# Four-tile pairs in another order of work, and an earlier table read on the DMA-issuing engine, in a ragged self-attention kernel

## The chip, the cores and the metric

The kernel runs on one core of one Trainium2 chip. The metric is device time in microseconds (us) for one execution. A core has a matrix engine (TensorE, PE), a vector engine (VectorE, DVE), a scalar engine (ScalarE, ACT), a general engine (GpSimd, POOL) and an engine that here only issues transfers (SyncE, SP). Each runs its own instruction stream; they meet through semaphores. PE writes only to PSUM, which this kernel divides into eight banks.

## The reference

32 sequences of 512 rows by 512 columns, each with a length between 64 and 511; 8 heads of 64 columns. Rows beyond a sequence's length are zero in the output.

```python
for b in range(batch):
    x_b = x[b, :lengths[b]]
    q, k, v = np.split(x_b @ w_qkv, 3, axis=-1)        # per head: (rows, 64)
    scores = scale * q @ k.T
    attn = softmax(scores)
    output[b, :lengths[b]] = (attn @ v)
```

The lengths are drawn once. Sorted and put in pairs, the longer length of each of the 16 pairs, rounded up to the next class (multiples of 32, and 340), is: 512, 448, 384, 352, 352, 340, 320, 288, 256, 224, 224, 192, 160, 160, 128, 96. In tiles of 128 rows that is four tiles for pairs 0 and 1, three for pairs 2 to 7, two for pairs 8 to 13 and one for pairs 14 and 15. No pair has class 480 or 416.

## The kernel before, in words

The sequences are sorted by length on the chip, and worked off in pairs from the longest. There is one straight piece of code per class and engine; a pair runs the code of its class, and branches lead from one class to the next. A body has two halves, `h` = 0 and 1. Half `h` does the attention of sequence `h` and, between its steps, the projections of the other buffer's sequence, that is of the one that comes next. Everything is done with two buffers of `xT`, `qkT`, `v_aug` and `onat`.

`half` (from L682) writes the order of a half out by hand, as a line of tokens. What they do:

- `S`: the scores of one pair of heads (a unit `i`, 0 to 3) against one 128-row tile of keys: two matmuls over 64 rows of the array (the two heads lie in the upper and the lower 64 rows), into one of two PSUM slots `s0`, `s1` in turn. ACT then writes the exponential to `ep` (L346) and frees the slot. The units come in the order 1, 2, 3, and 0 of the next sequence; with four tiles that is 16 `S`.
- `Qi`, `Ki`: a projection of unit `i` for the next sequence, four matmuls over 128 rows into one bank; capital letters let DVE move it to `qkT` (L410), small ones ACT (L409).
- `Ei` and then `Fi`, `Gi`, `Hi` or `Ii`: the same two projections, Q and K of unit `i`, in two banks at once, with matmuls over 64 rows: `E` (`cross_begin`) adds the upper rows into one bank and the lower rows into the other, the later token (`cross_end`) the rest. With `G`, DVE moves Q and ACT moves K.
- `Vi`: the value projection of row tile `i`, four matmuls of 512 columns over 128 rows; DVE moves it (L433).
- `Ai` (`attnv`): attention times values of unit `i`. DVE then takes the reciprocal of the row sums (L610) and multiplies (L629, L631) into `onat`. A `+` mixes its matmuls evenly into those of the token before.
- `O`: ACT issues the store of the first half of the columns. SP issues that of the second half.

A bank is free for the next writer once the engine that empties it has signalled; `acquire` puts that wait into PE's stream. Bodies with three tiles take the four banks `a0`, `a1`, `v0`, `v1` in turn (`in_turns`, L842), for projections and `A` alike. Bodies with four tiles use `a0`, `a1` for projections, and `v0` with `v1` together for `A`, in this order (L672):

```python
4: "S S Q0 +A0 S S K0 V0 S S Q1 +A1 S S K1 V1 S S Q2 +A2 S S K2 V2 S S Q3 +A3 S S V3 K3 O",
```

PE's bodies begin at chosen places of its instruction blocks (`align`, with the slots `FIRST` and `SECOND`), and hints announce branches.

SP's body of a class waits in each half until PE has begun it (`s_xtf`), issues the transposes of the next `x` into `xT[h]`, the store of the half before, and the load of an `x` five sequences ahead. Which sequences these are it reads from a small table, four registers a row (`read_step`, L1460). A body of two tiles has a branchless form for all but the last such pair (`steady`, L1464; pairs 8 to 12): one read at the top of the body (in `body`), and one between the halves (L1472).

Of the kernel before, what the change touches and what calls it, by code (L numbers as in the profile page):

```python
# [13 lines left out]
P = 128  # L14
NH = 8
HD = 64
# [7 lines left out]
SECOND = {4: 20, 3: AGAIN, 2: 0, 1: None}  # L24
AT_DENSE = 20
FIRST_DENSE = 4
PIECE = 266
PIECE_DENSE = 274
DENSE_ROWS = 340
# [121 lines left out]
def kernel(  # L151
# [9 lines left out]
    B, MAXS, D = x.shape  # L161
# [32 lines left out]
    rank = sb("rank", [B, 1], FP32)  # L194
# [11 lines left out]
    steps = sb("steps", [1, B, 4], I32)  # L206
# [4 lines left out]
    rcp = sb("rcp", [P, NPAIR, 4 * NPAIR], FP32)  # L211
# [332 lines left out]
            return  # L544
        group(pr, b, "dve", v_mms(b, h, i, T, of), v_out(b, h, i, T, of))

    def attnv(pr, h, i, T, late=False, b=None):

        for s_ in ("s0", "s1"):
            if pr.pair[s_] == i or T == 1 and pr.pair[s_] is not None:  # L550
                acquire(pr, s_)
        for v in halves_av if b is None else (b,):
            acquire(pr, v)
        va = v_aug[h]
        if b is not None:
            jobs = [(2 * 74 * qt, i, qt) for qt in range(T)]
        elif T == 1:
            jobs = [(74 * 2 * j, j, 0) for j in range(NPAIR)]
        elif T == 4:
            jobs = [(256 * qt, i, qt) for qt in range(T)]  # L560
        else:
            jobs = [(74 * (4 * qt + 2 * (i % 2)), i, qt) for qt in range(T)]
        mms = []
        for o0, j, qt in jobs:
            for par in range(2):
                o = o0 + par * (HD + 1 if T == 4 else 74)
                into = pav if b is None else area[b]
                for kt in range(T):
                    mms.append(
                        mm(  # L570
                            into[:, o : o + HD + 1],
                            ep[:, j, par, kt, qt * P : (qt + 1) * P],
                            va[:, kt, 2 * j + par, :],
                            kt == 0,
                            kt == T - 1,
                        )
                    )
        if b is None and T in (2, 3) and i % 2 == 0:
            acquire_carry(pr, mms)
            return  # L580
        on = onat[h]
        if b is not None:
            res = into[:, 0 : 2 * 74 * T].rearrange("p (t a d) -> p t a d", a=2, d=74)
            dst = on[:, i // 2, 0:T, P * (i % 2) : P * (i % 2 + 1)]
            dst = dst.rearrange("p t (a d) -> p t a d", d=HD)
            sh, fin = [T, 2], i % 2 == 1
        elif T == 4:
            res = pav.rearrange("p (j n) -> p j n", n=256)[:, :, 0 : 2 * (HD + 1)]
            res = res.rearrange("p j (a d) -> p j a d", d=HD + 1)
            dst = on[:, i // 2, :, P * (i % 2) : P * (i % 2 + 1)]  # L590
            dst = dst.rearrange("p t (a d) -> p t a d", d=HD)
            sh, fin = [NT, 2], i % 2 == 1
        else:
            sh, fin = [2, 4] if T == 1 else [T, 4], True
            res = pav[:, 0 : 74 * sh[0] * 4].rearrange("p (b j d) -> p b j d", j=4, d=74)
            if T == 1:
                dst = on[:, :, 0, :].rearrange("p b (j d) -> p b j d", d=HD)
            else:
                dst = on[:, i // 2, 0:T, :].rearrange("p t (a d) -> p t a d", d=HD)
        rv = rcp[:, i, 0 : sh[0] * sh[1]].rearrange("p (j a) -> p j a", a=sh[1])  # L600
        num, den = res[..., 0:HD], res[..., HD]
        name = "av" if b is None else b
        close(pr, name, "dve", mms, False)
        each = T == 4 or b is not None

        def recip():
            for j in (0, 1) if T == 1 else (i // 2,) if not each or i % 2 == 0 else ():
                pr.take("dve", s_od[h][j], 16)
            pr.take("dve", full[(name, "dve")])
            pr.add("dve", lambda e: e.reciprocal(out=rv, in_=den).then_inc(s_r, 1))  # L610

        def mult():
            pr.take("dve", s_r)

            if T == 1:
                cuts = [(slice(0, 2), 0)]
            elif h == 0:
                cuts = [(slice(0, T - 1), None), (slice(T - 1, T), T - 1)]
            else:
                cuts = [(slice(t, t + 1), t) for t in range(T)]  # L620

            def fn(e):
                for w, t in cuts:
                    ops = dict(
                        out=dst[:, w], in0=num[:, w],
                        in1=rv[:, w].unsqueeze(3).broadcast_to(list(num[:, w].shape)),
                    )
                    if t is None:
                        ins = e.tensor_tensor(op=ALU.mult, **ops)  # L629
                    else:  # L630
                        ins = e.scalar_tensor_tensor(  # L631
                            scalar=now[0][:, 1, t : t + 1], op0=ALU.mult, op1=ALU.mult, **ops
                        )
                if fin:
                    ins.then_inc(s_of[h][i // 2], 1)
                if b is not None:
                    if fin:
                        ins = e.memset(small, 0.0)
                    ins.then_inc(free[b], 1)

            pr.add("dve", fn)
            if b is not None:
                pr.busy[b] = True

        todo = {"R": recip, "X": mult}
        if not late:
            for fn in todo.values():
                fn()
        return todo
# [5 lines left out]
    def spread_last(pr):  # L655
# [15 lines left out]
    ORDER = {  # L671
# [3 lines left out]
    }  # L675
    DENSE = "K2 q2 D E1 E3 I1 H3 D k0 c A0 Q0~ A1 D V2 O V1 A2 D A3~ V0"

    def read_class(pr, h):
        for g in ("act", "dve") if h == 0 else ("pe",):
# [2 lines left out]
    def half(pr, h, T, N, W, st, last=False):  # L682
# [29 lines left out]
        units = [(i, k) for i in (1, 2, 3, 0) for k in range(per)]  # L712
        first, norm, dones, both = True, {}, 0, []
        dense, turns = is_dense(N), in_turns(N)
        toks = (DENSE if dense else ORDER[T]).split()

        def pick(second=False):
            if turns:
# [11 lines left out]
        for tok in toks:  # L730
            k = tok.lstrip("+")[0]
            over, tok = tok != tok.lstrip("+"), tok.lstrip("+")
            over2, tok = tok != tok.rstrip("~"), tok.rstrip("~")
            i = int(tok[1]) if len(tok) > 1 else 0
            if k in "SD" and turns:
                at = g if units[0][0] == 0 else h
# [10 lines left out]
            elif k == "D":  # L747
                i = units[0][0]
                del units[:T]
                scores_dense(pr, *((g, i, W) if i == 0 else (h, i, N)))  # L750
            elif k == "A":
                if first:
                    first = False
                    pr.take("pe", s_on[h])
# [1 line left out]
                if turns:  # L756
                    assert len(st["seen"]) == len(area), st["seen"]
                    for v in area:
                        if st["holds"].get(v) == (h, "V"):
                            acquire(pr, v)  # L760
                norm[i] = attnv(pr, h, i, T, f"X{i}" in toks, b)
                if turns:
                    give(b)
                if over:
# [74 lines left out]
    def is_dense(N):  # L839
        return -(-N // P) == 3 and 3 * N <= 2 * MAXS  # L840

    def in_turns(N):  # L842
        return -(-N // P) == 3 and (not is_dense(N) or "E" in DENSE)

    def make_body(N, W, last=False):

# [293 lines left out]
    def graph(e, name, opening=None, before=None):  # L1140
# [13 lines left out]
        def align(N, slots, off=0):  # L1154
            slot = slots[-(-N // P)]
            if slot == AGAIN and is_dense(N):
                slot = AT_DENSE
            elif slots is FIRST and is_dense(N):
                slot = FIRST_DENSE
            if fetch and slot is not None:  # L1160
                e.addr_align(FETCH, offset=(slot + off) % FETCH, max_nops=0)

# [158 lines left out]
    with nc.Block() as block:  # L1321

        @block.sync
        def _(e):
# [132 lines left out]
                    e.reg_mov(owed, 0)  # L1457
                nc.switch_bb(out_, parent=top)

            def read_step(h):  # L1460
                e.reg_load(steps_r[h], steps[
                    0:1, bass.ds(e.snap(rank, min_val=0, max_val=B - 1), 1), :])

            def steady(N):  # L1464

                k, top = CLASSES.index(N), nc.cur_bb
                yes, no = f"even_b{N}", f"even_x{N}"
                e.br_cmp(steps_r[0][3], CLASSES.index(P), yes, no, "IS_LT")
                nc.switch_bb(yes, parent=top)
                for h in range(2):  # L1470
                    if h:
                        read_step(h)  # L1472
                    wait_dec(e, s_xtf[h])
                    to_xT(h, N, 2)
                    if h == 0:
                        pay_owed(f"{N}e", False)
                    else:
                        pay(0)
                    wait_dec(e, s_xc[1 - h])
                    load(1 - h, 5, N, index(h, 0))  # L1480
                    e.reg_add(rank, rank, 1)
                e.reg_mov(owed, 1)
                e.reg_mov(flat, 1)
                e.br_cmp(cur, k, f"sp_b{k}", f"even_z{N}", "IS_EQ")
                nc.switch_bb(f"even_z{N}", parent=top)
                e.br(f"sp_x{k}")
                nc.switch_bb(no, parent=top)
# [325 lines left out]
```

## Time and profile before

| What | Value |
|---|---|
| Time, median of 3 runs | 341.05 us (338.79 to 342.54) |
| The profiled execution | 339.78 us |
| Its span, first to last instruction | 338.0 us |
| Granted TensorE clock | 0.996 |
| PE busy | 324.0 us, 96% |
| ACT busy | 240.0 us, 71% |
| DVE busy | 215.3 us, 64% |
| POOL busy | 63.2 us, 19% |
| Stretch of pair 1 (class 448, four tiles) | about 63.4 to 99.7 us |
| Stretch of pairs 8 to 12 (two tiles, branchless SP body) | about 239.5 to 306.8 us |

Times inside the profile count from the start of the span. Busy time of PE counts a matmul from its start to its modelled end, and matmuls overlap, so the distance between the starts of successive instructions says more than their duration. The two stretches were found by the shapes of the matmuls: a score matmul has as many columns as the pair's class.

### The profile page before, as it was taken

How to read it: one execution, taken by the hardware profiler on the slowest of the kernel's cores; microseconds unless marked ns; L12 is line 12 of the kernel's file. 1: busy time of each engine (PE TensorE's matmuls, PEld its weight loads, DVE VectorE, ACT ScalarE, POOL GpSimd, SP SyncE). 2: the span in 40 equal slices, each digit the busy share in tenths (PEclk: the TensorE clock that was granted, in tenths of full speed). 3: DMA queues.
4: the chain of work that ended last, by engine and by line, in shares of the span. 5: the costliest groups of instructions: out<-in, count | busy, mean ns of one | idle time of the engine just before them, and what ended most of it. 6: DMA issues, size and time to landing. Idle time of an engine off the chain costs nothing. (4 is left out here: it accounts for less than half of the span.)

```text
span 338.0 us, 12174 instructions
## 1 busy us (share of the span) xinstructions
PE 324.0 (96%) x4326; PEld 207.2 (61%) x4327; DVE 215.3 (64%) x580; ACT 240.0 (71%) x337; POOL 63.2 (19%) x102
## 2 busy tenths in 40 slices
PE   7899999999999999999999999999999999999991
PEld 2565544555545656556666676777677777676770
DVE  3576566666665576567567556765767667777672
ACT  4567887777769878877977887778775666555541
POOL 3634020202010210220220122012111211221340
PEclk9999999999999999999999999999999999999998
DMA  6956799966856976986787978697899657886732
GB/s 203 360 145 215 131 395 243 355 155 214 163 183 153 299 263 162 282 294 183 233 305 247 225 237 298 137 260 218 209 148 240 189 148 170 200 166 154 174 105 69
DMA packets 82273, 72.11 MB, mean 213 GB/s; under 512 B 40652, under 2 KB 63180, under 8 KB 82196
## 3 DMA queue, kind: packets, MB, share of 16 engines
q1 hardware_dynamic: 70340, 59.61, 66.7%
q10 hardware_dynamic: 11856, 11.54, 9.8%
q8 instruction: 40, 0.66, 0.8%
q14 instruction: 37, 0.30, 0.4%
HBM read 25.32 MB, written 36.70 MB: 183 GB/s over the span
## 5 line engine op out<-in xcount | busy, mean ns | idle before, releaser
L346 ACT ACTIVATE ep<-psc 128x704 f16<-128x704 f32 (+7 forms) x193 | 156.8, 858 | 60.2 <-PE psc L304 42.9
L304 PE MATMUL pa<-xT,w_r 128*128 128x224 f16 (+21 forms) x984 | 134.0, 276 | 3.0 <-PEq L59 1.3
L304 PEld LDWEIGHTS pa<-xT,w_r 128*128 128x128 f16 (+1 forms) x984 | 74.7, 97 | 35.5 <-issue 14.1
L410 DVE CAST qkT<-pa 128x448 f16<-128x448 f32 (+9 forms) x85 | 48.7, 574 | 47.1 <-PE pa L304 46.0
L304 PE MATMUL psc<-qkT 64*128 64x352 f16 (+17 forms) x702 | 66.9, 287 | 0.9 <-PEq L59 0.3
L304 PE MATMUL pa<-w_r,xT 128*128 128x512 f16 (+4 forms) x356 | 63.4, 333 | 0.6 <-DVE v_aug L531 0.5
L304 PE MATMUL pav<-v_aug,ep 128*128 128x65 f16 x1414 | 62.1, 194 | 0.2 <-PEq L59 0.2
L304 PEld LDWEIGHTS pav<-v_aug,ep 128*128 128x128 f16 x1414 | 55.4, 98 | 9.7 <-issue 1.4
L1652 POOL CAST v_aug<-masks 128x24 f16 (+4 forms) x33 | 9.1, 276 | 245.4 <-POOLq L1281 245.4
L631 DVE SCALAR_TENSOR_TENSOR onat<-pav,masks,rcp 128x128 f32<-128x128 f32 (+2 forms) x137 | 48.2, 391 | 5.6 <-DVE rcp L610 2.1
L378 ACT ACTIVATE ep<-psc 128x960 f16<-128x960 f32 (+3 forms) x48 | 43.3, 960 | 8.8 <-PE psc L304 6.0
L433 DVE TENSOR_TENSOR v_aug<-pa,masks 128x512 f16<-128x512 f32 (+1 forms) x52 | 34.8, 675 | 14.7 <-PE pa L304 13.8
L304 PE MATMUL pav<-xT,w_r 64*128 64x352 f16 (+10 forms) x328 | 43.6, 300 | 0.3 <-DVE v_aug L433 0.3
L1647 POOL CAST x<-x_nat 128x1536 f16<-128x1536 f32 (+3 forms) x33 | 42.0, 1274 | 9.2 <-POOLq L1281 8.4
L304 PEld LDWEIGHTS psc<-qkT 64*128 64x128 f16 x702 | 25.8, 94 | 29.0 <-issue 20.6
L304 PEld LDWEIGHTS pa<-w_r,xT 128*128 128x128 f16 (+2 forms) x356 | 24.9, 98 | 21.0 <-issue 4.8
L409 ACT CAST qkT<-pa 128x352 f16<-128x352 f32 (+7 forms) x58 | 26.4, 461 | 15.0 <-PE pa L304 8.0
L304 PEld LDWEIGHTS pav<-xT,w_r 64*128 64x128 f16 (+1 forms) x328 | 23.7, 95 | 10.0 <-issue 2.1
L610 DVE RECIPROCAL rcp<-pav 128x8 f32<-128x8 f32 (+1 forms) x71 | 14.0, 198 | 20.4 <-PE pav L304 15.7
L304 PE MATMUL pav<-w_r,xT 128*128 128x512 f16 (+3 forms) x100 | 19.3, 343 | 0.0
L304 PEld LDWEIGHTS pa<-v_aug,ep 128*128 128x128 f16 x378 | 13.5, 98 | 4.3 <-issue 1.8
L629 DVE TENSOR_TENSOR onat<-pav,rcp 128x256 f32<-128x256 f32 (+1 forms) x32 | 14.6, 457 | 1.1
(84 smaller groups left out, 146.4 us busy)
## 6 DMA issues: line engine op xcount, KB each, us to landing
out_dram<-zt SPq DMA_DIRECT2D x16, 768.0 KB, 6.1
x_nat<-in_x_dram SPq DMA_DIRECT2D x12, 512.0 KB
x_nat<-in_x_dram SPq DMA_DIRECT2D x5, 1024.0 KB
out_dram<-onat ACTq DMA_DIRECT2D x12, 384.0 KB, 5.4
out_dram<-onat SPq DMA_DIRECT2D x12, 384.0 KB, 4.7
x_nat<-in_x_dram SPq DMA_DIRECT2D x17, 256.0 KB, 6.3
out_dram<-onat ACTq DMA_DIRECT2D x16, 256.0 KB, 3.8
x_nat<-in_x_dram SPq DMA_DIRECT2D x4, 768.0 KB
```

The source lines that it names most:

```text
L304: return lambda e: e.matmul(o, lhsT, rhs, start=start, stop=stop)
L346: lambda e: e.activation(out=dst, in_=src, func=AF.Exp, scale=scale),
L378: lambda e, par=par, b=b: e.activation(out=ep[:, i, par, 0:3, 0:N], in_=psc_f[:, par, 0 : 3 * N].rearrange("p (t n) -> p t n", n=N), func= ...
L409: return lambda e: e.copy(out=dst, in_=src)
L410: return lambda e: e.tensor_copy(out=dst, in_=src)
L433: return lambda e: e.tensor_tensor(out=v_aug[h][:, t, lo // HD : lo // HD + n, 0:HD], in0=area[b][:, 0:w].rearrange("p (a d) -> p a d", d=HD),
L610: pr.add("dve", lambda e: e.reciprocal(out=rv, in_=den).then_inc(s_r, 1))
L629: ins = e.tensor_tensor(op=ALU.mult, **ops)
L631: ins = e.scalar_tensor_tensor(scalar=now[0][:, 1, t : t + 1], op0=ALU.mult, op1=ALU.mult, **ops)
L1647: e.tensor_copy(out=x16[h][:, 0:T, :], in_=x_nat[h][:, 0:T, :]).then_inc(s_xc[h], 1)
L1652: e.tensor_copy(out=v_aug[h][:, 0:T, :, HD], in_=src[:, 0, 0:T].unsqueeze(2).broadcast_to([P, T, NH]),).then_inc(s_on[h], 1)
```

## The change

Two edits that do not touch each other.

**Four tiles, 448 and 416 rows.** `in_turns` now holds for all classes over 256 and up to 448 rows, so these two classes take the four banks in turn too, and follow a new order, `FOUR`. In it Q and K are always projected together with 64-row matmuls (`E` and `G`), most of them between the first nine `S`; K is moved by ACT. `A` is cut in two: `Ai` does row tiles 0 and 1, and the new token `Zi` row tiles 2 and 3, each in a bank of its own with a reciprocal and multiplications of its own. PE's alignment slot for these classes becomes 4 in place of 20. Classes 512 and 480 keep the old order. Of the classes concerned, this input has one pair, pair 1.

**SP, two tiles.** In `steady` the row of the second half is read at the top of the body, into spare registers, right after the row of the first. Between the halves two register moves take the place of the read.

```diff
+FOUR_ROWS = 448
+AT_FOUR = 4
...
-    def attnv(pr, h, i, T, late=False, b=None):
+    def attnv(pr, h, i, T, late=False, b=None, qts=None):
...
-            jobs = [(2 * 74 * qt, i, qt) for qt in range(T)]
+            jobs = [(2 * 74 * k, i, qt) for k, qt in enumerate(qts)]
...
-            sh, fin = [T, 2], i % 2 == 1
+            sh, fin = [n, 2], i % 2 == 1 and T - 1 in qts
...
+            elif b is not None:
+                whole = [] if h else [k for k, t in enumerate(qts) if t < T - 1]
+                cuts = [(slice(0, len(whole)), None)] if whole else []
+                cuts += [(slice(k, k + 1), t) for k, t in enumerate(qts) if k not in whole]
...
+    FOUR = "S E1 S G1 S E2 S G2 S E0 S E3 S G0 G3 S S A0 Z0 V1 +A1 S S Z1 V3 +A2 S O S V0 +Z2 S A3 Z3 S S V2"
...
-        toks = (DENSE if dense else ORDER[T]).split()
+        toks = (DENSE if dense else FOUR if T == 4 and turns else ORDER[T]).split()
...
-            elif k == "A":
+            elif k in "AZ":
...
-                norm[i] = attnv(pr, h, i, T, f"X{i}" in toks, b)
+                cut = 2 if T == 4 and turns else T
+                qts = range(cut) if k == "A" else range(cut, T)
+                norm[i] = attnv(pr, h, i, T, f"X{i}" in toks, b, qts)
...
     def in_turns(N):
-        return -(-N // P) == 3 and (not is_dense(N) or "E" in DENSE)
+        return 2 * P < N <= FOUR_ROWS
...
+            elif 3 * P < N <= FOUR_ROWS:
+                slot = AT_FOUR
...
-            def read_step(h):
-                e.reg_load(steps_r[h], steps[
-                    0:1, bass.ds(e.snap(rank, min_val=0, max_val=B - 1), 1), :])
+            def read_step(h, at=None, into=None):
+                at = rank if at is None else at
+                e.reg_load(into or steps_r[h], steps[
+                    0:1, bass.ds(e.snap(at, min_val=0, max_val=B - 1), 1), :])
+
+            second = [e.alloc_register(f"{r}_second") for r in ("ahead", "own", "steady", "rank")]
...
                 nc.switch_bb(yes, parent=top)
+                e.reg_add(second[3], rank, 1)
+                read_step(1, second[3], [second[0], cur] + second[1:3])
                 for h in range(2):
                     if h:
-                        read_step(h)
+                        for k_, r in ((0, second[0]), (2, second[1])):
+                            e.reg_mov(steps_r[1][k_], r)
                     wait_dec(e, s_xtf[h])
                     to_xT(h, N, 2)
```

More of the change, by code (lines that the diff above doesn't have):

```diff
@@ L565, in attnv @@
             for par in range(2):
-                o = o0 + par * (HD + 1 if T == 4 else 74)
+                o = o0 + par * (HD + 1 if T == 4 and b is None else 74)
                 into = pav if b is None else area[b]
@@ L582, in attnv @@
         if b is not None:
-            res = into[:, 0 : 2 * 74 * T].rearrange("p (t a d) -> p t a d", a=2, d=74)
-            dst = on[:, i // 2, 0:T, P * (i % 2) : P * (i % 2 + 1)]
+            n = len(qts)
+            res = into[:, 0 : 2 * 74 * n].rearrange("p (t a d) -> p t a d", a=2, d=74)
+            dst = on[:, i // 2, qts[0] : qts[0] + n, P * (i % 2) : P * (i % 2 + 1)]
             dst = dst.rearrange("p t (a d) -> p t a d", d=HD)
-            sh, fin = [T, 2], i % 2 == 1
+            sh, fin = [n, 2], i % 2 == 1 and T - 1 in qts
         elif T == 4:
@@ L599, in attnv @@
                 dst = on[:, i // 2, 0:T, :].rearrange("p t (a d) -> p t a d", d=HD)
-        rv = rcp[:, i, 0 : sh[0] * sh[1]].rearrange("p (j a) -> p j a", a=sh[1])
+        r0 = 2 * qts[0] if b is not None else 0
+        rv = rcp[:, i, r0 : r0 + sh[0] * sh[1]].rearrange("p (j a) -> p j a", a=sh[1])
         num, den = res[..., 0:HD], res[..., HD]
@@ L606, in recip @@
         def recip():
-            for j in (0, 1) if T == 1 else (i // 2,) if not each or i % 2 == 0 else ():
+            opens = i % 2 == 0 and (b is None or 0 in qts)
+            for j in (0, 1) if T == 1 else (i // 2,) if not each or opens else ():
                 pr.take("dve", s_od[h][j], 16)
```

## The prediction

> **What bounds the kernel now.** I read the page's busy lines first.
>
> ```profile
> span 338.0 us, 12174 instructions
> ```
> ```profile
> PE 324.0 (96%) x4326; PEld 207.2 (61%) x4327; DVE 215.3 (64%) x580; ACT 240.0 (71%) x337; POOL 63.2 (19%) x102
> ```
>
> Then the busy time by stretch, for what the change touches: pair 1's two halves, and pairs 8 to 12.
>
> ```profile
> core 0: us, PE busy (x) PEld busy (x) DVE busy (x) ACT busy (x) POOL busy (x), PEclk, DMA share, GB/s
> 63.40:81.70 18.30, 18.18 (x211) 9.47 (x212) 11.62 (x25) 13.88 (x17) 2.23 (x2) 1.00 0.64 194
> 81.70:99.70 18.00, 17.70 (x210) 9.39 (x210) 12.29 (x34) 13.59 (x16) 2.19 (x2) 1.00 0.72 184
> 239.50:306.80 67.30, 65.94 (x901) 49.33 (x900) 47.07 (x114) 42.39 (x61) 12.99 (x20) 1.00 0.81 184
> ```
>
> PE fills all three: 18.18 of 18.30 us, 17.70 of 18.00, 65.94 of 67.30, at the full clock. So only PE's own pace and its few gaps are worth anything here; ACT (13.9 of 18.3) and DVE (11.6) have room in pair 1. The rest of the kernel keeps its code, so the change can move 36 us directly, and 67 through SP. Next, PE's timeline in pair 1, to see where its pace is lost.
>
> ```profile
> 65.13 0.41 PE L304 MATMUL pav<-v_aug,ep 128*128 128x65 f16 x8
> 65.38 0.35 PE L304 MATMUL pa<-xT,w_r 128*128 128x448 f16 x1
> 65.56 0.41 PE L304 MATMUL pav<-v_aug,ep 128*128 128x65 f16 x8
> 65.90 0.55 PE L304 MATMUL psc<-qkT 64*128 64x448 f16 x4
> 66.39 0.93 PE L304 MATMUL pa<-xT,w_r 128*128 128x448 f16 x4
> 67.16 1.03 PE L304 MATMUL pa<-w_r,xT 128*128 128x512 f16 x4
> 68.11 0.55 PE L304 MATMUL psc<-qkT 64*128 64x448 f16 x4
> ```
>
> The columns are start, duration, form, count. Starts tell the pace. Four projection matmuls of 448 columns take 0.77 us (66.39 to 67.16), 0.19 each. The four score matmuls run two at a time, so they should take 0.38, but the next thing starts after 0.49: 0.11 lost on leaving the 64-row matmuls. Eight `A` matmuls take 0.25 (65.13 to 65.38), but 0.34 ahead of the scores (65.56 to 65.90): 0.09 lost on entering them. I take **0.19 us per group of 64-row matmuls** (the gaps add to 0.20; entries after a `V` look slightly shorter). A half has eight such groups, 1.5 us.
>
> **Part 1: pair 1 in the new order.** First, whether 64-row projections lose anything. Pair 2, with 384 rows, has them among its scores:
>
> ```profile
> 101.90 0.32 PE L304 MATMUL pav<-xT,w_r 64*128 64x384 f16 x1
> 102.06 0.33 PE L304 MATMUL psc<-qkT 64*128 64x384 f16 x2
> ...
> 102.22 0.32 PE L304 MATMUL pav<-xT,w_r 64*128 64x384 f16 x1
> ```
>
> A pair of them, and a pair of scores, each take 0.16 us, with nothing lost between: 384 columns at the same pace as 448 in 0.19. `E` and `G` together are eight such pairs where Q and K were eight single matmuls of the same length. So PE's streaming work is unchanged, 32 `A` matmuls a unit included, and only the groups count. In the new line the runs of 64-row work are: first `S` to the ninth (with all `E` and `G`), `S S` after `A1`, `S S` around `O`, `S` after `Z2`, `S S` before `V2`. Five groups in place of eight: **-3 x 0.19 = -0.57 us per half.**
>
> Then the seams, where a half starts against banks that the code before leaves busy.
>
> ```profile
> 63.63 0.66 DVE L410 CAST qkT<-pa 128x480 f16<-128x480 f32 x1
> ```
> ```profile
> 63.41 0.55 PE L304 MATMUL psc<-qkT 64*128 64x448 f16 x4
> 64.08 0.35 PE L304 MATMUL pa<-xT,w_r 128*128 128x448 f16 x1
> ```
> ```profile
> 98.93 0.68 DVE L433 TENSOR_TENSOR v_aug<-pa,masks 128x512 f16<-128x512 f32 x1
> ...
> 99.67 0.50 PE L304 MATMUL pa<-xT,w_r 128*128 128x384 f16 x2 [0.30 <-DVE v_aug L433]
> ```
>
> *Entry from pair 0.* That pair keeps the old order and ends with `V3 K3` in `a0` and `a1`. The old first projection needs one of them and starts at 64.08, which is 0.18 after the usual 0.49 of two `S`. `E1` needs both, after a single `S`, so it could start at 63.41 + 0.19 = 63.60, but DVE empties K3's bank until 63.63 + 0.66 = 64.29; with the 0.06 that a release takes (98.93 + 0.68 to 99.67), 64.35. A wait of **+0.75** is new, and the old delay of 0.18 falls inside it. First half: -0.57 + 0.75 - 0.18 = **0.0**.
>
> *Exit to pair 2.* Its first projection waits 0.30 for the bank of the last `V3`. In the new order the last four bank uses are `Z2`, `A3`, `Z3`, `V2`; the next body starts with `a0`, that of `Z2`, given up four tokens earlier. **-0.30.** Between the halves there is no wait: `E1` meets the banks of `Z2` and `A3`, with `Z3 S S V2` in between. Second half: -0.57 - 0.30 = **-0.87**.
>
> *ACT, the cover.* K's four moves go to ACT.
>
> ```profile
> L346 ACT ACTIVATE ep<-psc 128x896 f16<-128x896 f32 x44 | 38.1, 914 | 16.0 <-PE psc L304 14.0 <-ACTq L59 2.0
> ...
> L409 ACT CAST qkT<-pa 128x448 f16<-128x448 f32 x8 | 4.3, 533 | 0.9 <-PE pa L304 0.4 <-ACTq L59 0.4
> ```
> ```profile
> 79.88 1.73 ACT L346 ACTIVATE ep<-psc 128x896 f16<-128x896 f32 x2 [0.60 <-PE psc L304]
> ```
> ```profile
> 103.95 0.47 ACT L409 CAST qkT<-pa 128x384 f16<-128x384 f32 x1
> 104.31 0.50 ACT L409 CAST qkT<-pav 128x384 f16<-128x384 f32 x1
> ```
>
> Back to back, an exponential takes 1.73 - 0.91 = 0.82, a move of 384 columns 0.36, so about 0.42 for 448 (estimate, by columns). Over a half that is 16 x 0.82 + 4 x 0.42 = 14.8 of some 17.5 us. The tight part is the front: nine `S` and eight `E`/`G` take PE 9 x 0.19 + 8 x 0.76 = 7.8 us and ACT 9 x 0.82 + 4 x 0.42 = 9.1. PE may be two exponentials (1.64) ahead, so ACT reaches the point at which the ninth `S` has its slot at 7.5: under 7.8, no wait, with 0.3 to spare. It then catches up during `A0 Z0 V1 +A1`, which asks nothing of it. At the uncovered durations, 0.914 and 0.533, the same point comes at 10.4 - 1.8 = 8.6, a wait of 0.8 a half; so this term lies between 0 and +1.6, and I take **0**, since the exponentials of the nearest row do overlap.
>
> *DVE* gives up four moves a half, each a little under the 0.66 us that 480 columns took above, and gains four reciprocals of some 0.2 and a shorter multiply per unit: at most as much as it loses, out of 11.6 of 18.3. Nothing. The store by SP now waits for `Z3`, after the half's end; SP's transposes slip by under a microsecond, and they have a whole half of 17 us to land.
>
> **Part 2: SP in pairs 8 to 12.** The reads, and the end of the last wait before the transposes, as single instructions:
>
> ```profile
> L1461 SPq TENSOR_LOAD <-steps x32: 300/547/993, 40.8 to 327.9; - x32
> L1481 SPq FUSED_REGOPS  x5: 133/137/144, 246.3 to 300.5; - x5
> ```
> ```profile
> L1461 SPq TENSOR_LOAD <-steps x1: 307/307/307, 267.3 to 267.3; - x1
> L1281 SPq EVENT_SEMAPHORE  x3: 17/17/17, 264.9 to 268.4; - x3
> ```
>
> A read in this stage takes 0.31 us and its address 0.14: the second read adds **0.45** at the top. In pair 10 the read ends at 267.6 and the wait for PE at 268.4, so it is hidden. By the same two rows of the other bodies there is 0.3 to spare in pair 11 and nothing in 8, 9 and 12; their first transposes go out up to 0.45 later. What that costs is read where PE needs `xT`; pair 8 has the least to spare:
>
> ```profile
> L1366 SPq DMA_TRANSPOSE xT<-x x2: 1256/1629/2002, 241.9 to 244.0; - x2
> ...
> DMA to landing us min/median/max: 2.9/3.8/4.6
> ```
> ```profile
> 247.56 0.56 PE L304 MATMUL pa<-xT,w_r 128*128 128x224 f16 x4
> ```
>
> The second lands at 244.0 + 2.9 = 246.9 (4.6 would be later than its use), 0.66 before PE reads it. 0.45 fits. So **0**, with +0.5 at the other end if the second read takes the longest time of the row, 0.99. Between the halves SP saves the read, but waits there for PE anyhow, save in pair 12:
>
> ```profile
> L1461 SPq TENSOR_LOAD <-steps x1: 963/963/963, 300.6 to 300.6; - x1
> ```
>
> This one ended after PE's signal, so those transposes may go out earlier, by less than the read's 0.96. PE shows no wait for them now; gain 0, at most 0.3 by my estimate.
>
> [...]
>
> **Sum**: 0.0 - 0.87 + 0 = -0.9 us. The profiled execution, 339.78 us (span 338.0 and 1.8 around it), becomes 338.9. It lies 1.27 below the median of 341.05; from that median, **340.2 us**.
>
> **The rivals.**
> 1. *ACT sets the pace in pair 1.* For it: the front has only 0.3 us to spare, and K's move stands behind an exponential that itself waits for PE. Against it: the overlap seen at 79.88. It costs 0.8 a half: -0.9 + 1.6 = +0.7, 341.8.
> 2. *SP's transposes come late* (the one on the slower side): each top of a two-tile body passes its 0.45 to PE, five times 0.45 = 2.25, net +1.35, 342.4. It decides where landing is less than 0.45 ahead of use: 0.66 in pair 8. For it: the DMA engines are 81% busy in this stretch, and transposes take very different times to land:
>
> ```profile
> DMA to landing us min/median/max: 2.4/3.4/6.3
> ```
>
>    Against it: PE shows no wait for `xT` now.
> 3. *The change does not do what the order suggests:* the 0.19 belongs to waits that stand ahead of each group, not to the kind of matmul; then regrouping gives nothing, only the seams count, +0.57 - 0.30 = +0.3, 341.3. Against it: the seamless 0.16 of pair 2, whose `E` waits for banks too.
> 4. [...] PE's branches sometimes stall its sequencer:
>
> ```profile
> L1208 PEldq COMPARE_BRANCH  x13: 73/86/672, 24.1 to 331.2; - x13
> ```
>
> A half gets 64 more PE instructions, so the branches after each half lie elsewhere in their blocks. Two stalls of 0.67 that are not covered: +0.4, 341.5. [...]
>
> **How the numbers follow.** Forecast 0.55 (339.7 to 340.8 by itself), rival 1 0.15, rival 2 0.1, rival 3 0.12, rival 4 0.08. All lie within 1%, 3.4 us, which is about what a measurement of this kernel can tell from no change: the three runs before lie 3.75 us apart. The range takes in rival 2 above, and below the forecast with pair 12's 0.3 and without the entry wait (-0.75), 339.1, less about 1 us for the scatter of a median: 338.0 to 342.6. Faster by over 1% needs such scatter on top of the best case (0.06), slower rival 2 with more than five late bodies or with rival 1 (0.07).
>
> **What would show it.** In the profile after: one unbroken run of 64-row matmuls at 0.19 us a pair from `E1` on, pair 1 shorter by 0.9 us, all of it in the second half; a wait of about 0.75 before the first `E1`, for DVE's move of K3; no wait at pair 2's start. Rival 1 would show as waits of the seventh to ninth `S` for ACT, rival 2 as gaps before the first projection of halves in pairs 8 to 12, rival 3 as 0.1 us gaps between `S` and `E`, rival 4 as idle time at 81 or 99 us with no releaser but the sequencer. I am wrong if pair 1 gets longer, or if the stretch of pairs 8 to 12 changes by more than 0.5 us.

## The result and the profile after

| | before | after |
|---|---|---|
| Time, median (22 runs each, side by side) | 340.60 us (338.46 to 343.28) | 339.31 us (338.37 to 341.01) |
| Ratio after / before, 95% interval | | 0.9956 (0.9937 to 0.9974) |
| The profiled execution, and its span | 339.78, 338.0 us | 338.68, 336.7 us |
| Pair 1, first half | 18.27 us | 18.48 us |
| Pair 1, second half | 17.99 us | 17.29 us |
| Pairs 2 to 7 | 139.85 us | 139.67 us |
| Pairs 8 to 12 | 67.32 us | 67.27 us |
| Pair 13 | 12.40 us | 12.56 us |
| The one-tile pairs, to the end | 18.78 us | 18.17 us |

The ratio says -1.5 us (-0.9 to -2.1). The lengths of the stretches are differences between the starts of the first matmuls of each (for the one-tile pairs, of the eighth matmul of their first projections, the same one in every run); they are compared in this way all through. Pair 1 gives 0.48 of the 1.3 us that lie between the two spans; the one-tile pairs, whose code is the same, give 0.61.

On the page of after PE is busy 322.9 us (96%), DVE 212.9 (63%) and ACT 243.0 (72%). The busy time by stretch, for the two halves of pair 1:

```profile
core 0: us, PE busy (x) PEld busy (x) DVE busy (x) ACT busy (x) POOL busy (x), PEclk, DMA share, GB/s
63.28:81.76 18.48, 17.82 (x242) 9.89 (x242) 10.15 (x31) 14.88 (x21) 2.13 (x2) 1.00 0.71 219
81.76:99.05 17.29, 17.24 (x241) 10.04 (x241) 10.42 (x32) 14.82 (x21) 2.12 (x2) 1.00 0.63 187
```

In the second half PE now has 0.05 us without work, so what is left there is PE's own pace. The first half has 0.66 idle: one wait. ACT goes from 13.9 and 13.6 us to 14.9 and 14.8 and still isn't the bound. PE's timeline of after (start, duration, form, count, and in brackets the idle time before and what ended it) shows the entry, the seam between the halves, and the exit:

```profile
63.28 0.36 PE L306 MATMUL psc<-qkT 64*128 64x448 f16 x2
64.30 0.93 PE L306 MATMUL pa<-xT,w_r 64*128 64x448 f16 x8 [0.66 <-DVE qkT L412]
65.06 0.37 PE L306 MATMUL psc<-qkT 64*128 64x448 f16 x2
65.31 0.93 PE L306 MATMUL pa<-xT,w_r 64*128 64x448 f16 x8
66.08 0.35 PE L306 MATMUL psc<-qkT 64*128 64x448 f16 x2
66.27 0.92 PE L306 MATMUL pav<-xT,w_r 64*128 64x448 f16 x8
...
81.76 0.36 PE L306 MATMUL psc<-qkT 64*128 64x448 f16 x2
81.96 0.87 PE L306 MATMUL pa<-xT,w_r 64*128 64x416 f16 x8
82.66 0.35 PE L306 MATMUL psc<-qkT 64*128 64x448 f16 x2
82.92 0.88 PE L306 MATMUL pa<-xT,w_r 64*128 64x416 f16 x8
83.84 0.36 PE L306 MATMUL psc<-qkT 64*128 64x448 f16 x2
...
98.18 1.04 PE L306 MATMUL pav<-w_r,xT 128*128 128x512 f16 x4
99.05 0.81 PE L306 MATMUL pa<-xT,w_r 128*128 128x384 f16 x4
```

Read the starts. `E1` comes 1.02 us after the first `S` (63.28 to 64.30), 0.83 more than the 0.19 that a score alone takes. After it the run of 64-row matmuls goes on unbroken: eight take 0.76 (64.30 to 65.06), a score takes 0.19 (66.08 to 66.27). But the scores ahead of a `G` take 0.25 (65.06 to 65.31; 82.66 to 82.92), and `G1` of the second half takes 0.92 (82.92 to 83.84) where `E1` took 0.70. Pair 2 starts at 99.05 with nothing to wait for.

DVE's timeline gives the reason for the entry: it moves K3 of pair 0 until 64.16, as it did before the change.

```profile
63.50 0.66 DVE L412 CAST qkT<-pa 128x480 f16<-128x480 f32 x1
```

PE's weight loads show what a `G` waits for (its own `E`, whose sums it continues), and the table read in PE's own instruction stream sits where `G1` of the second half is long:

```profile
65.31 0.49 PEld L306 LDWEIGHTS pa<-xT,w_r 64*128 64x128 f16 x8 [0.32 <-PE pa L306]
```
```profile
L1124 PEldq TENSOR_LOAD <-cls x1: 691/691/691, 83.1 to 83.1; - x1
```

### The profile page after: what moved, and what is told of

It reads as the page before. It is cut to its first block, busy times and chain, and to the rows that moved or that the text cites. A ratio compares the mean times of both kernels' runs of the same rounds, so it can differ in the third digit from the quotient of the medians.

```text
span 336.7 us, 12340 instructions
## 1 busy us (share of the span) xinstructions
PE 322.9 (96%) x4390; PEld 208.6 (62%) x4391; DVE 212.9 (63%) x588; ACT 243.0 (72%) x345; POOL 63.3 (19%) x102
## 5 line engine op out<-in xcount | busy, mean ns | idle before, releaser
L306 PE MATMUL pa<-xT,w_r 128*128 128x224 f16 (+21 forms) x984 | 122.7, 276 | 3.0 <-PEq L61 1.3
L412 DVE CAST qkT<-pa 128x512 f16<-128x512 f32 (+9 forms) x73 | 41.5, 569 | 43.6 <-PE pa L306 42.7
L306 PE MATMUL pav<-v_aug,ep 128*128 128x65 f16 x1254 | 55.0, 194 | 0.1
L306 PEld LDWEIGHTS pav<-v_aug,ep 128*128 128x128 f16 x1254 | 49.0, 98 | 8.8 <-issue 1.3
L306 PE MATMUL pav<-xT,w_r 64*128 64x352 f16 (+12 forms) x392 | 50.8, 307 | 0.3 <-DVE v_aug L435 0.3
L435 DVE TENSOR_TENSOR v_aug<-pa,masks 128x512 f16<-128x512 f32 (+1 forms) x46 | 30.7, 673 | 14.2 <-PE pa L306 13.6
L411 ACT CAST qkT<-pa 128x352 f16<-128x352 f32 (+8 forms) x62 | 28.7, 467 | 13.4 <-PE pa L306 6.5
L306 PE MATMUL pav<-w_r,xT 128*128 128x512 f16 (+3 forms) x124 | 26.9, 350 | 0.0
L615 DVE RECIPROCAL rcp<-pav 128x8 f32<-128x8 f32 (+2 forms) x69 | 13.5, 196 | 20.0 <-PE pav L306 15.3
L306 PEld LDWEIGHTS pa<-v_aug,ep 128*128 128x128 f16 x538 | 19.6, 98 | 7.1 <-issue 2.9
L306 PE MATMUL pa<-v_aug,ep 128*128 128x65 f16 x538 | 22.3, 194 | 0.0
```

The lines of the kernel that those rows point to most:

```text
L306: return lambda e: e.matmul(o, lhsT, rhs, start=start, stop=stop)
L411: return lambda e: e.copy(out=dst, in_=src)
L412: return lambda e: e.tensor_copy(out=dst, in_=src)
L435: return lambda e: e.tensor_tensor(out=v_aug[h][:, t, lo // HD : lo // HD + n, 0:HD], in0=area[b][:, 0:w].rearrange("p (a d) -> p a d", d=HD),
```

## The experiments

Those on the order of work (`four_...`) keep SP's old read between the halves; those on SP (`sp_only`, `sp_late`, `sp_mid`) keep the old order. A single time tells little, since the times of before beside these runs lie some 4 us apart; for the experiments with one run the stretch lengths count.

**One edit at a time: `four_only`, `sp_only`.** The first is the change without SP's edit (the read between the halves is back), the second without the new order, which is this edit of after:

```diff
-FOUR_ROWS = 448
+FOUR_ROWS = 384
```

> The new order of pair 1 alone; SP reads its second row between the halves as before. Theory A (all of the gain comes from pair 1, and SP's edit is worth nothing): the same time as with both edits, ratio to before about 0.9956 to 0.998, and the same pair 1, 35.8 us from its first score matmul to pair 2's first projection. Theory B (a good part of the measured 1.5 us comes from SP's edit, since pair 1 became only 0.5 us shorter in the profile): ratio about 0.9985, with the higher and more scattered runs of before (338.5 to 343.3) instead of the narrow ones of after (338.4 to 341.0).

> SP's edit alone; pair 1 in the old order. Theory A: no change, ratio 0.999 to 1.001, and the scatter of before. Theory B: ratio about 0.997, and runs that scatter as little as those of after. If the second read at the top makes transposes late that PE needs, slower, by up to 2 us.

| | time | before beside it | ratio (95%) | pair 1 | pairs 8 to 12 |
|---|---|---|---|---|---|
| `four_only` | 339.02 | 339.92 | 0.9967 (0.9943 to 0.9991) | 35.75 | 67.32 |
| `sp_only` | 339.84 | | 0.9993 (0.9961 to 1.0025) | 36.25 | 67.26 |

The new order alone gives pair 1 the length it has in after (35.77; before 36.25). SP's edit alone gives nothing that the times can tell from none, and pairs 8 to 12 change by 0.06. `sp_only` is also the test of rival 2, since its early read was a slow one. SP's rows in pair 8, by line, with shortest, median and longest time in ns, and then PE's first use of those transposes:

```profile
L1476 SPq TENSOR_LOAD <-steps x2: 312/426/539, 240.7 to 241.3; - x2
```
```profile
L1380 SPq DMA_TRANSPOSE xT<-x x2: 1253/1380/1507, 242.0 to 243.6; - x2
...
DMA to landing us min/median/max: 2.6/3.0/3.5
```
```profile
247.14 0.94 PE L306 MATMUL pa<-xT,w_r 128*128 128x224 f16 x8
```

The second read took 0.54 there, and with its address SP lost 0.67 us, as much as the 0.66 to spare that the prediction read. The second transpose still landed at 246.2 (issued at 243.6, landing 2.6 us later), 0.9 ahead of its use at 247.14. By how much more SP could be late, this run doesn't show.

**The alignment slot: `four_slot20`.** As `four_only`, with the slot that the four-tile bodies had before:

```diff
-AT_FOUR = 4
+AT_FOUR = 20
```

> As the new order alone, but with the old alignment slot 20 for the classes 448 and 416. If the place of the code in its blocks matters (rival 4 of the prediction), PE idles for 0.3 to 1.3 us at the start, the middle or the end of pair 1 with no releaser but its sequencer; if not, the same as the new order alone within 0.2 us in pair 1.

346.31 us, ratio 1.0172 (1.0123 to 1.022): **slower than before by 5.8 us** (4.2 to 7.5), and than `four_only` by 7.3. Pair 1 takes 42.04 us, 6.3 more than with slot 4, and pairs 2 to 7 1.4 more. PE's timeline, at the seam and at pair 2's start, and then busy times by stretch with PE's clock (the columns as above, the clock in the third place from the end):

```profile
81.11 1.04 PE L306 MATMUL pav<-w_r,xT 128*128 128x512 f16 x4
84.13 0.36 PE L306 MATMUL psc<-qkT 64*128 64x448 f16 x2 [1.98 <-issue]
...
102.02 1.04 PE L306 MATMUL pav<-w_r,xT 128*128 128x512 f16 x4
105.64 1.44 PE L306 MATMUL pa<-xT,w_r 128*128 128x384 f16 x4 [2.59 <-PEq L61]
```
```profile
84.40:85.33 0.93, 0.93 (x11) 0.52 (x10) 0.00 (x0) 0.77 (x1) 0.33 (x2) 0.75 0.20 63
85.33:87.09 1.76, 1.76 (x13) 0.81 (x10) 0.00 (x0) 1.06 (x2) 1.76 (x1) 0.50 0.38 75
```

The four matmuls at 81.11 end the half and take 0.97 in after; here the next half starts after 3.02, and pair 2 after 3.62 in place of 0.87. That is 2.05 + 2.75 = 4.8 us. PE's branches stand in both gaps. Their rows (ns, and when they start), at the end of the first half (L1263) and of the second (L1222), with slot 20 and then in after with slot 4:

```profile
L1263 PEldq COMPARE_BRANCH  x1: 3433/3433/3433, 80.6 to 80.6; - x1
L1222 PEldq COMPARE_BRANCH  x1: 3321/3321/3321, 102.2 to 102.2; - x1
```
```profile
L1263 PEldq COMPARE_BRANCH  x1: 360/360/360, 80.3 to 80.3; - x1
L1222 PEldq COMPARE_BRANCH  x1: 451/451/451, 98.1 to 98.1; - x1
```

With each gap the clock is granted at 0.50 for a while. By the rows it falls from full at about 84.9 (0.75 on average up to 85.33), and it is back at 88.3 (0.77 on average from 88.00 to 88.60); the second time it is at 0.50 from 105.3 to 108.8 (0.82 on average from 104.20 to 106.00, 0.66 from 106.00 to 110.00). That is 3.4 us each time, worth about 1.5: the first of them makes up the rest of pair 1's 6.3, the second the 1.4 of pairs 2 to 7. This is rival 4, branches that stall PE's sequencer, at a price far above the one it was given. The new slot is what keeps it away.

**What a group of 64-row matmuls costs: `four_wide`.** Q and K as whole 128-row projections among the same scores, fourteen more groups in pair 1; slot 20, with which this body shows no stall:

```diff
-    FOUR = "S E1 S G1 S E2 S G2 S E0 S E3 S G0 G3 S S A0 ...
+    FOUR = "S Q1 S k1 S Q2 S k2 S Q0 S Q3 S k0 k3 S S A0 ...
```

> The new order alone, but with Q and K projected over 128 rows, at the same places and in the same banks (slot 20, since the code is as long as the old). If changing between 64-row and 128-row matmuls costs 0.19 us per group, as the prediction has it, pair 1 has twelve groups a half in place of five: 2 x 7 x 0.19 = 2.7 us more, less some 0.6 at the entry, where the first projection needs one bank only; pair 1 about 37.8 us instead of 35.8. If the 0.19 belongs to the waits ahead of a group (rival 3), about 35.2.

341.52 us in one run; pair 1 37.41 us, +1.66. PE's timeline:

```profile
64.44 0.36 PE L306 MATMUL psc<-qkT 64*128 64x448 f16 x2
64.74 0.93 PE L306 MATMUL pa<-xT,w_r 128*128 128x448 f16 x4
65.60 0.36 PE L306 MATMUL psc<-qkT 64*128 64x448 f16 x2
```

No wait stands anywhere in these rows, and yet a score takes 0.30 (0.19 in the unbroken run) and four matmuls of a projection 0.86 (0.77): 0.20 us for one change to 64-row matmuls and back. Fourteen of them make 2.8; less the entry's 0.83 and the four waits of `G` (0.06 each), which this order doesn't have, that is +1.7, as measured. Nor is it a wait too short for the brackets: the slot that the third score, at 66.76, goes into was free from 65.79, when ACT's exponential of the first ended. The 0.19 belongs to the kind of matmul, and rival 3 falls.

**Who moves K: `four_dve`.** `F` in place of `G`, so DVE moves it:

```diff
-    FOUR = "S E1 S G1 S E2 S G2 S E0 S E3 S G0 G3 ...
+    FOUR = "S E1 S F1 S E2 S F2 S E0 S E3 S F0 F3 ...
```

> The new order alone, with K moved by DVE instead of ACT: four moves of 0.42 us a half less for ACT. In the profile after, pair 1 is 0.4 us longer than the prediction's sum. If that is ACT holding up scores at the front (rival 1 in small), the second half shrinks from 17.3 to about 17.0 and pair 1 to 35.3 to 35.5 us; if ACT has nothing to do with it, 35.75 stays.

343.11 us in one run; pair 1 37.19, **longer** by 1.44 where the expectation has it shorter or the same. PE now waits for DVE's moves, first here:

```profile
72.31 1.16 PE L306 MATMUL pa<-v_aug,ep 128*128 128x65 f16 x32
73.67 0.38 PE L306 MATMUL pav<-w_r,xT 128*128 128x512 f16 x1 [0.19 <-DVE qkT L412]
```

`A0` with `Z0`, 32 matmuls, takes 1.36 us to the next start; in after it takes 1.00. `E3` and the second half show the same. The long `G1` of the second half stays, at 0.91, so ACT wasn't its cause. Moving K by ACT is a part that the new order needs, not one that could be left out.

**Two scores ahead of `E1`: `four_ss`.**

```diff
-    FOUR = "S E1 S G1 S E2 S G2 S E0 S E3 S G0 G3 S S A0 Z0 ...
+    FOUR = "S S E1 S G1 S E2 S G2 E0 S E3 S G0 S G3 S A0 Z0 ...
```

> The new order alone, with two scores ahead of E1 instead of one. The wait for DVE's move of K3 at the entry (0.66 us in the profile after) shrinks by one score pair, 0.19, and ACT gets its second exponential earlier in both halves: pair 1 about 35.4 us. If the entry wait is not what it seems, 35.75.

340.72 us in one run; pair 1 36.32, longer by 0.57 where I had expected it shorter. PE's timeline, at the start of both halves:

```profile
64.15 0.55 PE L306 MATMUL psc<-qkT 64*128 64x448 f16 x4
65.17 0.93 PE L306 MATMUL pa<-xT,w_r 64*128 64x448 f16 x8 [0.47 <-DVE qkT L412]
...
82.51 0.36 PE L306 MATMUL psc<-qkT 64*128 64x448 f16 x2
83.24 0.36 PE L306 MATMUL psc<-qkT 64*128 64x448 f16 x2 [0.37 <-ACT ep L348]
```

`E1` still starts 1.02 after the first `S`: K3's bank comes free when DVE is done, and the second score only fills part of that wait. In the second half a second `S` so early meets a slot that ACT hasn't emptied. So the entry depends on which bank `E1` takes, which the next run changes.

**Another bank for `E1`: `four_turn`.** `E1` begins in `v0` and `v1`, after a wait for V3's bank, which DVE empties first; the turn is set back by two banks before `V0` of the second half:

```diff
+            if T == 4 and turns and h == 0 and tok == "E1":
+                acquire(pr, "a0")
+            if T == 4 and turns and h == 1 and tok == "V0":
+                st["banks"] = st["banks"][2:] + st["banks"][:2]
...
+        if T == 4 and in_turns(N):
+            st["banks"] = ["v0", "v1", "a0", "a1"]
```

> The new order alone, with the banks taken in another turn: E1 of the first half takes v0 and v1 and waits only until DVE has emptied the bank of V3 (one move, 0.66 us, earlier than that of K3); in the second half the turn goes back before V0, so that pair 2 starts as before. The entry wait nearly goes: pair 1 35.1 to 35.3 us, ratio about 0.995 to 0.9965 against 0.9967 of the new order alone. If the turn back costs a wait for a bank in the second half, part of this is lost.

340.28 us, ratio 1.0012 (0.9986 to 1.0038); pair 1 36.40. PE's timeline:

```profile
63.55 0.36 PE L306 MATMUL psc<-qkT 64*128 64x448 f16 x2
64.07 0.93 PE L306 MATMUL pav<-xT,w_r 64*128 64x448 f16 x8 [0.15 <-PEq L61]
...
94.20 0.54 PE L306 MATMUL psc<-qkT 64*128 64x448 f16 x4
95.81 0.38 PE L306 MATMUL pav<-w_r,xT 128*128 128x512 f16 x1 [1.08 <-PEq L61]
```

The entry comes down from 1.02 to 0.52, and the first half to 17.98 us, as expected. But setting the turn back makes `V0` meet a bank that was given out only just before: 1.61 from the scores to `V0`, 0.47 in after. What was won at the entry is paid twice at `V0`.

**All three mended: `best`, and one of them alone: `after_c`.** `best` is after with that entry, with the turn kept and set right at the end (`Z3` and `V2` of the second half take the second bank), and with PE's table read moved from the second half's `G1` to just ahead of `A0` (token `c`). `after_c` has the moved read alone.

```diff
-    FOUR = "... S G0 G3 S S A0 Z0 ...
+    FOUR = "... S G0 G3 S S c A0 Z0 ...
...
+            if T == 4 and turns and h == 0 and tok == "E1":
+                acquire(pr, "a0")
+            over2 = over2 or T == 4 and turns and h == 1 and tok in ("Z3", "V2")
...
+        if T == 4 and in_turns(N):
+            st["banks"] = ["v0", "v1", "a0", "a1"]
```

> Both edits of the change, with the two waits found in pair 1 taken away: E1 of the first half takes v0 and v1 and waits for the bank of V3 alone (0.5 us, shown by the run with the banks in another turn; the way back is now made by Z3 and V2 of the second half taking the second bank in the turn, where a bank is free), and PE's read of the class table moves from after G1 to before A0. Pair 1 from 35.8 to 35.0 to 35.3 us; ratio to before 0.993 to 0.996.

> The changed kernel with nothing but the class read moved to before A0, on PE, ACT and DVE. If the 0.23 us by which the first G of the second half is longer than the other three (0.93 against 0.70) is PE's own read, 0.69 us there, it goes and pair 1 is 35.5 us; if it is ACT's exponentials that hold up the score after it, it stays at 35.77.

`best`: 339.01 us, ratio 0.9967 (0.9943 to 0.9992), pair 1 35.45. `after_c`: 338.33 in one run, pair 1 35.80. PE's timeline of `best`, then of `after_c`:

```profile
63.17 0.36 PE L306 MATMUL psc<-qkT 64*128 64x448 f16 x2
63.68 0.93 PE L306 MATMUL pav<-xT,w_r 64*128 64x448 f16 x8
```
```profile
82.62 0.88 PE L306 MATMUL pa<-xT,w_r 64*128 64x416 f16 x8
83.34 0.35 PE L306 MATMUL psc<-qkT 64*128 64x448 f16 x2
...
88.67 0.54 PE L306 MATMUL psc<-qkT 64*128 64x448 f16 x4
89.32 1.14 PE L306 MATMUL pa<-v_aug,ep 128*128 128x65 f16 x32
```

`best` keeps the short entry (0.51) and pays 0.14 at `Z3` (0.64 from the start of `A3` to that of `Z3`, 0.50 in after): pair 1 is 0.32 shorter than in after. In time it can't be told from after. In `after_c`, `G1` is down from 0.92 to 0.72, so that long `G1` was the table read; but the two scores ahead of `A0` now take 0.65 in place of 0.48. In both places the read costs some 0.2 us; PE has only 0.05 us without work in this half of after.

**Later transposes: `sp_late`, `sp_mid`, `sp_last`.** Three reads more at the top of the bodies of pairs 8 to 12, three more between their halves, and, on top of after, eight more ahead of pair 13's halves. The edit of the first:

```diff
+                for _ in range(3):
+                    e.reg_load(second[:3] + [tmp], steps[
+                        0:1, bass.ds(e.snap(second[3], min_val=0, max_val=B - 1), 1), :])
```

> Old order in pair 1, and SP reads its table three times more at the top of a two-tile body, with the read between the halves kept: transposes at the top go out some 1.2 us later than before in pairs 8, 9 and 12, and 0.5 to 1.2 later in 10 and 11. By the prediction's margins only pair 8 (0.66 us) and perhaps 11 (1.0) run out, so PE loses about 0.5 us in pair 8 and little elsewhere, ratio about 1.002. If each late top passes to PE in full (rival 2), 4 to 6 us, ratio 1.012 to 1.017. If nothing happens, the two-tile bodies have more to spare than I read.

> The kernel before, with SP reading its table three times more between the halves of the two-tile bodies (some 1.2 us): the other side of what the change removes there. If a read between the halves costs nothing, because SP waits for PE there and the transposes land early enough, pairs 8 to 12 stay at 67.3 us. If the saved read is worth something, they grow by more than 0.3 us, and by up to 1 us for each body in which SP was on the path.

> The changed kernel with eight reads more (some 3 us) in the last two-tile body only, pair 13, which has no branchless form and which the change does not touch. In the profiles so far the stretch after pair 13 takes 18.1 to 21.9 us for the same code, and it is long where SP's reads or transposes there are slow. If SP is on the path in this stretch, it grows by 2 us or more over 18.2, and the time by as much; then the scatter of the runs comes from there, and a read taken off the two-tile bodies ahead could help there. If not, it stays.

These three did less than their expectations say. Nothing uses the registers that the added reads fill, and the reads aren't in the trace: SP does 32 reads of this table in each of them, as in before. Only the computing of their addresses is left, 0.05 to 0.13 us each and 0.1 apart. So `sp_late` made SP's first transposes of pair 8 later by 0.38 us (0.60 after the branch in place of 0.22) and not by a microsecond, `sp_mid` added some 0.3 us, `sp_last` 0.77. None says anything about the price of a read.

| | time | ratio (95%) | pairs 8 to 12 | one-tile pairs |
|---|---|---|---|---|
| `sp_late` | 341.18 | 1.0011 (0.9979 to 1.0044) | 67.27 | 20.46 |
| `sp_mid` | 340.99, one run | | 67.33 | 20.52 |
| `sp_last` | 340.25 | 0.9971 (0.9937 to 1.0005) | 67.16 | 20.41 |

With those smaller delays pairs 8 to 12 are unchanged. PE's largest wait there, in `sp_late`:

```profile
PE pa L306 <- PEq L61: 0.9, 3, 0.3
```

(total, count and longest, in us; it is no wait for transposes, and before has the same three, 0.8 in all). The last column is another matter, taken up at the end.

## Why the prediction was right, and where it was off

The forecast, -0.9 us and 340.2 from the median then known, is inside what was measured (-0.9 to -2.1), at its small end; so are "within 1%" and the range. That the number holds is in part luck: pair 1, from which all of it was to come, gives 0.48 us, half of the 0.9. The rest of the measured difference lies where the forecast has nothing, in these two profiles mostly in the one-tile pairs. By its steps:

- **Three groups of 64-row matmuls fewer a half, -0.57.** Right, in mechanism and size: `four_wide` puts a group at 0.20, and no gap opens in the run of after.
- **The entry, +0.75.** Right: 0.83, and its cause, DVE's move of K3, is the releaser in the row; `four_turn` and `best` take 0.5 of it away by taking another bank.
- **The exit, -0.30.** Right in its mechanism: pair 2 starts straight behind `V2`. Its size was mis-read. The 0.30 is the idle time in brackets, which counts from the modelled end of the matmuls before; by starts, as in most of the sum, the last projection of before takes 1.17 (98.50 to 99.67), and one that nothing waits behind 0.72:

```profile
93.25 0.88 PE L304 MATMUL pa<-xT,w_r 128*128 128x416 f16 x4
93.97 1.03 PE L304 MATMUL pa<-w_r,xT 128*128 128x512 f16 x4
...
98.50 0.87 PE L304 MATMUL pa<-xT,w_r 128*128 128x416 f16 x4
```

So the wait that the new order takes away was worth 0.45, 0.15 more than forecast.
- **First half 0.0, second -0.87.** The places are right, the sum is not: +0.21 and -0.70, together -0.48. Besides the exit, the term that was mis-sized is PE's unchanged streaming work, which I took to run on "with nothing lost between". Two things are lost. The four `G` that follow their own `E` after a single score wait for its sums, 0.06 each, 0.25 together with rounding. And PE's table read falls into the run in the second half: 0.22 on `G1` (0.92 for 0.70). Pair 2, on which I leaned, shows pairs of `E` alone, not a `G` so close behind its `E`. With 0.08 more at the entry, and the 0.15 of the exit, the sum is -0.87 + 0.25 + 0.22 + 0.08 - 0.15 = -0.47, as measured.
- **ACT as cover, 0.** Right, inside its 0 to +1.6: no score of the run waits for ACT in after. Rival 1 didn't happen.
- **DVE, nothing.** Its busy time in pair 1 falls from 23.9 to 20.6 us. It was worth more than "nothing" in one way: with K left to DVE, pair 1 is 1.44 longer.
- **SP, 0.** Right: 67.27 against 67.32, and 0.9993 (0.9961 to 1.0025) by itself. Rival 2 falls for one read more, even a slow one.
- **Rival 3** falls by `four_wide`: 0.20 us a group, where no wait stands in the rows.
- **Rival 4** didn't happen in the change but is real. I priced it from the longest branch of before, 0.67 us, and got two stalls, 1.3 us, which made +0.4 in all. `four_slot20` shows two of 3.3 to 3.4 us, with the half clock behind them, and +5.8 against before. That would have put the time outside the range; the step that failed is its price: none of the branches of before showed what such a stall can reach.

**What stays open.** Pair 1's 0.48 us is less than the 0.9 at which the interval of the main comparison begins, though inside that of `four_only` (0.3 to 1.9). The lowest times of before and after are alike, 338.46 and 338.37. Between the two profiles most of the rest lies in the one-tile pairs, whose code is unchanged and whose length differs from run to run by more than this (below). Whether the change makes their longer form rarer, no run here shows.

## What to carry to other kernels

When PE is full, count how often it changes from 128-row to 64-row matmuls and back, 0.2 us for each such group here, before looking for idle time. Price a wait by the distance between starts, since the idle column counts from modelled ends and shows less (0.30 for 0.45 here). Then check each seam, because a reordered body can lose at its entry what its inside gains, and the bank that it takes first decides that (`E1` 1.02 us after the first `S`, or 0.52 with another bank). The alignment slot is tried anew with each new order: here it weighed over ten times what the order itself did (6.3 us against 0.5). And look in the trace for the work that an experiment adds: a read whose result nothing uses may not be there.

## What the runs showed of the hardware that I had not expected

**A stalled branch costs more than its own time.** In `four_slot20` the two branches took 3.43 and 3.32 us, of which PE stood idle 1.98 and 2.59. What held them isn't shown: the slot is all that sets this run apart from `four_only`, and the instruction queues moved three packets between 78 and 92 us, against two in after, where nothing stalls.

With each gap the clock was granted at 0.50 for 3.4 us. The length of the gap alone does not decide it: 1.98 and 2.59 us here, and 1.99 at the end of `four_dve` (the mean clock of its profiled run is 0.990), were followed by 0.50; 2.18 in `four_only` (mean clock 0.996) was not. What does decide it, so few gaps don't show.

**The end of the kernel scatters.** The one-tile pairs take 18.0 to 21.9 us in these runs, with the same code. In nearly all the long ones PE stands idle for 0.4 to 2.2 us, for the same thing. PE's and POOL's timelines of `four_only`, and the transposes that SP issues for that tile (the first) and the next:

```profile
321.80 0.40 PE L306 MATMUL psc<-qkT 64*128 64x128 f16 x8
324.37 0.80 PE L306 MATMUL pa<-xT,w_r 128*128 128x96 f16 x15 [2.18 <-PEq L61]
```
```profile
323.62 0.61 POOL L1712 COPY xT<-xT 128x512 f16<-128x512 f16 x1 [3.51 <-POOLq L1295]
```
```profile
L1517 SPq DMA_TRANSPOSE xT<-x x2: 1191/1218/1246, 319.0 to 322.7; - x2
```

PE waits for POOL's copy of `xT`, and that for the first of these transposes, which landed 4.4 us after it was issued at 319.0. For all runs, in us, with the issue counted from pair 13's start:

| | issued after | landing took | PE's gap |
|---|---|---|---|
| the eight runs without the gap (before 10.6 and 2.6; after 10.9 and 3.3) | 10.4 to 11.1 | 2.4 to 3.3 | none |
| `four_turn` | 11.3 | 3.7 | 0.4 |
| `sp_late` | 11.6 | 5.3 | 1.8 |
| `four_dve` | 11.8 | 4.6 | 2.0 |
| `sp_mid` | 12.0 | 4.1 | 1.3 |
| `sp_last` | 12.1 | 4.3 | 1.8 |
| `four_only` | 12.3 | 4.4 | 2.2 |

Both parts go with the gap: the issue comes up to 1.4 us later than in after, and the landing takes up to 2.0 longer; in `sp_late` the landing is the greater part. What made SP late differs: a read of 0.8 to 0.9 us in the middle of pair 13 where after has 0.31 (`sp_last` and `four_only`), transposes that took 2.1 us to issue and not 1.6 (`four_only`), and in `sp_last` also the 0.77 that was added. What made the landing long, and whether a late issue does, the runs don't show. `four_dve` is the longest, at 21.9 us; there the clock of 0.50 followed the gap. So these transposes are on the path at the end of the kernel, and not in pairs 8 to 12; what a late SP costs there by itself isn't shown. `sp_only` is an exception: 19.28 us without this gap. That this scatter makes up the spread of the times is likely, but the runs without a profile don't show it.
